# Weight tiles that begin where the activations begin, and four other starts for the seven products

## The chip, the cores and the metric

The kernel runs on one core of a Trainium2 chip. The metric is the device time of one execution in microseconds. The kernel before has a median of 2064.72 us over 3 runs (2064.69 to 2067.99).

## The reference

Two layers of a decoder trunk work on 512 tokens of width 1024 in float32. Each layer has three sub-layers between RMS norms: a SwiGLU FFN of width 2816, a mixer with a gated linear recurrence and a windowed attention, and a second FFN.

```python
for l in range(DEPTH):
    gn = norm_gains[l]
    h = rms_norm(x, gn[0])
    x = x + 0.5 * rms_norm(swiglu(h, w_ffn1_gate[l], w_ffn1_up[l], w_ffn1_down[l]), gn[1])
    h = rms_norm(x, gn[2])
    proj = h @ w_in[l]
    ...
    y_hg = hgrn2_mixer(hq, hf, hi, hg, lb_all[l], hgrn_head_gain[l]) @ w_branch_hgrn[l]
    y_at = swa_sink_attention(aq, ak, av, attn_sinks[l]) @ w_branch_attn[l]
    mixed = jax.nn.sigmoid(gate_a) * y_hg + jax.nn.sigmoid(gate_b) * y_at
    x = x + rms_norm(mixed @ w_out[l], gn[3])
    h = rms_norm(x, gn[4])
    x = x + 0.5 * rms_norm(swiglu(h, w_ffn2_gate[l], w_ffn2_up[l], w_ffn2_down[l]), gn[5])
```

`swiglu(h, g, u, d)` is `(silu(h @ g) * (h @ u)) @ d`. Nearly all of the arithmetic is in these products with weights.

## The kernel before

**Precision.** The matmul engine takes its operands as `float32r`, which rounds a float32. So every operand is split into two parts: `hi` is the rounded value, and `lo` is what rounding left over. A product is then three matmuls that add up in one accumulator (`mm3`): stationary hi with moving hi, stationary hi with moving lo, stationary lo with moving hi. All three go through `mm` on line 114, which is why the profile puts them on one line.

**Tiles.** Activations lie in `s` tiles (`big()`, line 62), 61 slots of 128 partitions by 2048 bytes. Weights arrive from memory in `w` tiles of 128 by 1024 elements. A *weight item* is one such tile, or a sum of parts of two, split into a `whi` and a `wlo` tile. There are six slots for each of these two, of 4096 bytes in a partition. Constants have a pool of their own, `cp`, that lies ahead of all of these. A tile keeps its place in the partition, and a slot is handed on in rotation, so a tile's address modulo 256 follows from what is allocated ahead of it.

**The stream of weights.** `Stream` (line 156) holds the list of all items in the order in which they are used. `split` (line 322) and `quarter` (line 255) make an item: ScalarE copies the weight to `hi`; `lo` is then made in one of two ways. Either VectorE subtracts (`wlo` on lines 294 and 362), or ScalarE writes the negative of the weight to `lo` (line 357) and a transfer issued by GpSimd adds the weight to `hi`'s negative in place (line 360). The kinds of item are:

- `u`, `v`: one plain tile. In most of its uses a 128-column block of it is the stationary operand, and 512 columns of activations stream. In the `rows` items of the down projections and of the output projection it is the other way round: activations are stationary, and 512 columns of weights stream.
- `a`, `b`, `c`, `d`: made by `pairs` out of two tiles. They serve `sevenths` (line 1031), which computes a 2 by 2 block product with seven block products instead of eight. There a weight block is stationary and 256 columns of activations stream. Four of these items hold the seven weight blocks of a pair: `a`, `b` and `c` two each, and `d` one.
- `p1` to `p7`: the quarter items of the down projections, where the same scheme is used with weights streaming, 512 columns at a time.

An FFN begins with a few columns done plainly (`quad`, `project`), goes on with pairs (`fast`, line 1074), and ends with `down`. The first FFN has 15 pairs, each of the other three has 19. A pair is 84 matmuls of 256 columns. The mixers use `pairs` through `gates` (line 186), four pairs in each layer. `ahead` (line 372) makes items up to four ahead of the one in use, never more than six at a time, and TensorE's program order is written out by hand. A matmul waits for its weight load, and that waits for the item.

**Constants that the change touches.** `gh` and `grows` (lines 1544 and 1552) hold the norms' gains while they are turned into rows, once, early in the program. `lbmx` holds a maximum for the recurrence's lower bounds. The activation on line 138 makes ScalarE load its function before it is needed; its result, in a tile named `warm`, is not used.

The item as it is made before:

```python
it.hi = sb.tile([P, D], F32R, tag="whi", name=nm("whi"), bufs=WS)
it.lo = sb.tile([P, D], F32R, tag="wlo", name=nm("wlo"), bufs=WS)
```

Of the kernel before, what the change touches and what calls it, by code (L numbers as in the profile page):

```python
# [8 lines left out]
F32R = mybir.dt.float32r  # L9
I32 = mybir.dt.int32  # L10
AF = mybir.ActivationFunctionType
# [4 lines left out]
P = 128  # L16
D = 1024
S = 512
DEPTH = 2
KT = D // P  # L20
TT = S // P
D_FF = 2816
FT = D_FF // P
H = 4
# [12 lines left out]
W32, WS, AHEAD, TAIL, FIRST, EARLY, LATE = 4, 6, 3, 4, 7, 4, 8  # L37
TURN = 0
SEVEN = 16
ORDER = ("p1", "p3", "p7", "p2", "p6", "p5")  # L40
HEADS = (0, 4, 1, 5, 2, 6, 3, 7)

# [2 lines left out]
def trunk(ctx: ExitStack, tc: tile.TileContext, xin, wall, gains, lbT, hgain, sinks, c_dist, c_mask, c_ident, out):  # L45
    nc = tc.nc
    cp = ctx.enter_context(tc.tile_pool(name="cp", bufs=1))
    sb = ctx.enter_context(tc.tile_pool(name="sb", bufs=1))
# [9 lines left out]
    def nm(s):  # L58
        seq[0] += 1
        return f"{s}_{seq[0]}"  # L60

    def big(dt=F32, shape=None):
        return sb.tile(shape or [P, S], dt, tag="s", name=nm("s"), bufs=SLOTS)

    def small(shape, tag, bufs=4, dt=F32):
        return sb.tile(shape, dt, tag=tag, name=nm(tag), bufs=bufs)
# [7 lines left out]
    def const(shape, name, dt=F32):  # L74
        return cp.tile(shape, dt, tag=name, name=name)
# [3 lines left out]
    class Order:  # L79
        def __init__(self):  # L80
            self.t = 0.0
            self.rest = 0.0
            self.cos = []
# [51 lines left out]
    nc.vector.memset(ones, 1.0)  # L135
    eps_t = const([P, 1], "eps_t")
    nc.vector.memset(eps_t, EPS)
    nc.scalar.activation(out=small([P, 1], "warm", 2), in_=eps_t, func=AF.Copy, scale=eps_t)


    p = aux()
# [8 lines left out]
    class Item:  # L150


        def __init__(self, kind, u, left=8):
            self.kind, self.u, self.left = kind, u, left

    class Stream:
        def __init__(self):
# [16 lines left out]
            self.n += n  # L174
            self.wall += n

        def pairs(self, n):

            for _ in range(n):
                self.items += [Item("a", self.n), Item("b", self.n), Item("c", self.n), Item("d", self.n, 4)]  # L180
                for i in range(2):
                    self.src.setdefault(self.n + i, self.wall + i)
                self.n += 2
                self.wall += 2
# [70 lines left out]
        def quarter(self, it):  # L255

            q, u, v, h = it.q, it.u, it.u + it.n, (slice(0, S), slice(S, D))

            def sums(o, x, y, op):
                for c in range(2):  # L260
                    pin(nc.vector.tensor_tensor(o[c], x[c], y[c], op=op))  # L261

            def raw(i):
                self.load(i + 1)
                return [self.raw[i][:, c] for c in h]

            def leave(i):
                self.raw.pop(i)
                self.freed += 1
                self.load(self.freed + W32)  # L270

            if it.kind in ("p1", "p2"):
                w = raw((u if it.kind == "p1" else v) + q)
            elif it.kind in ("p3", "p5"):
                w = self.b22[q]
            elif it.kind == "p7":

                w = self.b12[q]
                if q == 0:
                    sums(w, w, self.b22[q], ALU.add)  # L280
            else:
                w = self.b12[q]
            it.hi = sb.tile([P, D], F32R, tag="whi", name=nm("whi"), bufs=WS)
            it.lo = sb.tile([P, D], F32R, tag="wlo", name=nm("wlo"), bufs=WS)
            for c in range(2):
                i = nc.scalar.copy(it.hi[:, h[c]], w[c])  # L286
                if self.pinned:
                    pin(i)
            if it.kind == "p7" and q + 1 < it.n:
                sums(self.b12[q + 1], self.b12[q + 1], self.b22[q + 1], ALU.add)  # L290
            elif it.kind == "p6":
                sums(self.b22[q], self.b22[q], w, ALU.add)
            for c in range(2):
                pin(nc.vector.tensor_tensor(it.lo[:, h[c]], w[c], it.hi[:, h[c]].bitcast(F32), op=ALU.subtract))  # L294
            if it.kind == "p7":

                sums(w, raw(u + q), w, ALU.subtract)
                leave(u + q)
            elif it.kind == "p5":
                self.b22[q] = None  # L300
                if q + 1 < it.n:
                    sums(self.b12[q], raw(v + q), self.b12[q], ALU.add)
                    leave(v + q)
            elif it.kind == "p4":
                self.b12[q] = None
                if q == 0:
                    i = it.n - 1
                    sums(self.b12[i], raw(v + i), self.b12[i], ALU.add)
                    leave(v + i)
            self.done += 1  # L310
            self.flight += 1
# [10 lines left out]
        def split(self):  # L322
            it = self.items[self.done]
            if it.kind[0] == "p":
                return self.quarter(it)
            u, last = it.u, it.kind in "uvd"
            self.load(u + (1 if it.kind in "uv" else 2))
            it.hi = sb.tile([P, D], F32R, tag="whi", name=nm("whi"), bufs=WS)
            it.lo = sb.tile([P, D], F32R, tag="wlo", name=nm("wlo"), bufs=WS)
            w, h = self.raw[u], (slice(0, D // 2), slice(D // 2, D))  # L330
            cols = (slice(0, D),)
            if it.kind == "u" and u < 2:
                cols = h
            if it.kind in "bcd":
                v = self.raw[u + 1]
            if it.kind == "b":

                self.t13 = sb.tile([P, D], F32, tag="tt", name=nm("tt"), bufs=2)
                pin(nc.vector.tensor_tensor(self.t13[:, h[0]], w[:, h[0]], v[:, h[0]], op=ALU.add))
                pin(nc.vector.tensor_tensor(self.t13[:, h[1]], v[:, h[0]], v[:, h[1]], op=ALU.add))  # L340
                w = self.t13
                self.product()
            elif it.kind == "c":

                t = sb.tile([P, D], F32, tag="tt", name=nm("tt"), bufs=2)
                pin(nc.vector.tensor_tensor(t[:, h[0]], self.t13[:, h[0]], v[:, h[1]], op=ALU.add))
                pin(nc.vector.tensor_tensor(t[:, h[1]], t[:, h[0]], w[:, h[1]], op=ALU.add))  # L347
                w = t
            elif it.kind == "d":
                w = v  # L350
                cols = h[1:]
            for c in cols:
                i = nc.scalar.copy(it.hi[:, c], w[:, c])  # L353
                if u < 6 or self.pinned or self.tight:
                    pin(i)
                if it.kind in "vad":
                    i = nc.scalar.mul(it.lo[:, c], w[:, c], -1.0)  # L357
                    if self.pinned or self.tight:
                        pin(i)
                    nc.gpsimd.dma_start(it.lo[:, c].bitcast(F32), w[:, c], accum_op=ALU.add)  # L360
                else:
                    self.hold(nc.vector.tensor_tensor(it.lo[:, c], w[:, c], it.hi[:, c].bitcast(F32), op=ALU.subtract))  # L362
            self.done += 1
            self.flight += 1
            if last:
                nu = u + (1 if it.kind in "uv" else 2)
                for i in range(u, nu):
                    self.raw.pop(i)
                    self.freed += 1
                self.load(self.freed + W32)  # L370
# [38 lines left out]
    ws = Stream()  # L409
# [1064 lines left out]
    for l in range(DEPTH):  # L1474
        for n in (0, 2, 4):
            if n == 2:
                ws.plain(4, "v")
                ws.plain(2 * H + 2 + 8 + LATE * 3 // 2)
                for _ in range(KT - LATE // 2):
                    ws.gates()  # L1480
                ws.rows(KT, False)
            else:
                p = FIRST if l + n == 0 else 3
                ws.plain(4, "v" if l and not n else "u")
                ws.plain(min(2 * p, 8) - 4)
                ws.plain(max(2 * p - 8, 0), "v")
                ws.pairs(FT - p)
                ws.rows(FT, True)
    pre = First()
    for k in range(KT):  # L1490
# [27 lines left out]
        pre.square(k)  # L1518
    lb = const([P, DEPTH, H], "lb")
    oml = const([P, DEPTH, H], "oml")  # L1520
    mx = const([P, H], "lbmx")
    ex = const([P, DEPTH, H], "lbex")
    sm = const([P, H], "lbsm")
    cum = const([P, H], "lbcum")
# [1 line left out]
    def gain_rows():  # L1526
# [14 lines left out]
        nc.vector.tensor_tensor(cum, ex[:, 0, :], ex[:, 1, :], op=ALU.add)  # L1541
        nc.vector.tensor_tensor(lb[:, 1, :], cum, ex[:, 0, :], op=ALU.subtract)
        nc.vector.tensor_scalar(oml, lb, -1.0, 1.0, op0=ALU.mult, op1=ALU.add)
        t = const([P, DEPTH, 6, KT], "gh")
        pin(nc.vector.tensor_scalar(t, g_sb, 1.0, None, op0=ALU.mult))
        for n in (1, 5):
            nc.vector.tensor_scalar(t[:, :, n, :], t[:, :, n, :], 0.5, None, op0=ALU.mult)
# [1 line left out]
        p = aux()  # L1549
        nr = DEPTH * 6 * KT  # L1550
        transpose(p[:nr, :P], t.rearrange("p a b c -> p (a b c)"))
        r = const([nr, P], "grows")
        nc.scalar.copy(r, p[:nr, :P])
        nc.sync.dma_start(rows_d, r)

# [88 lines left out]
```

## Time and profile before

| | |
|---|---|
| median of 3 runs | 2064.72 us |
| the profiled execution | 2063.08 us |
| its span, first to last instruction | 2061.3 us |
| mean granted clock of the matmul engine | 0.999 |
| matmuls, weight loads | 13531 each |
| matmuls that read a weight tile | 12096 |
| read from memory | 213.43 MB |

The profile names the engines PE (matmuls), PEld (the loads of stationary operands, which run beside the matmuls), DVE (VectorE), ACT (ScalarE), POOL (GpSimd) and SP (transfers). A row of groups gives line, engine, operation, the tile written, the tiles read, partitions and shape, the count, the busy time in us and the mean duration of one in ns, and then the idle time ahead of them with what ended it. For matmuls the stationary size comes as 128*128 and the streamed one behind it; `acc` and `aux` are accumulators, and "acc<-s,whi" means that `s` streams against a loaded `whi`, "acc<-whi,s" the reverse. A row of waits gives who waited, for whom, the total in us, how often, and the longest. A row of windows gives a stretch of the span, its length, the busy time and count, the granted clock and the load on the transfers. A row of the timeline gives start, length, engine, line and operation; "x2" means that two in a row are merged. Times in windows and timeline count from the start of the span.

### The profile page before, as it was taken

To read this page: it belongs to the slowest core of one execution; us is meant where nothing else is said; L and a number is where in the kernel's file an instruction comes from. 1 tells how busy PE (TensorE), PEld (TensorE's weight loads), DVE (VectorE), ACT (ScalarE), POOL (GpSimd) and SP (SyncE) were. 2 spreads that over 40 slices of the span, in tenths; PEclk is the share of its full clock that TensorE was granted. 3 is DMA by queue.
4 is the path that set the end of the run, shared out by engine and by line. 5 is a ranking of instruction groups with operands and counts; after the bars stand their busy time and mean duration, and the time that the engine had idled before them with its cause. 6 is when DMAs were issued, how large, how long until landed. Compare 5 with 4: busy or idle time off the path is not lost. (4 is left out here: it accounts for less than half of the span.)

```text
span 2061.3 us, 36501 instructions
## 1 busy us (share of the span) xinstructions
PE 2047.5 (99%) x13531; PEld 1818.4 (88%) x13531; DVE 1625.6 (79%) x2894; ACT 1252.2 (61%) x2213; POOL 268.2 (13%) x318
## 2 busy tenths in 40 slices
PE   9999999999999999999999999999999999999998
PEld 7899988877888899997899998888778989999977
DVE  5887888767777787888988878987676858788888
ACT  7566687447355556657866666864554545666684
POOL 0111141000000011113201111400000100111140
PEclk9999999999999999999999999999999999999999
DMA  8587797321237358778757888872122563778794
GB/s 253 148 189 189 171 206 222 125 72 62 81 94 210 116 135 193 190 197 204 193 161 184 189 193 204 176 232 91 62 72 62 136 192 95 184 188 189 187 197 123
DMA packets 166802, 328.07 MB, mean 159 GB/s; under 512 B 19072, under 2 KB 85088, under 8 KB 166624
## 3 DMA queue, kind: packets, MB, share of 16 engines
q1 hardware_dynamic: 122416, 228.16, 33.0%
q0 software_dynamic: 44064, 97.54, 28.5%
q8 instruction: 106, 1.74, 0.4%
q14 instruction: 72, 0.59, 0.1%
q10 hardware_dynamic: 144, 0.05, 0.0%
HBM read 213.43 MB, written 14.73 MB: 111 GB/s over the span
## 5 line engine op out<-in xcount | busy, mean ns | idle before, releaser
L114 PE MATMUL acc<-s,whi 128*128 128x256 f32 (+1 forms) x4976 | 1030.4, 306 | 0.4 <-ACT whi L353 0.4
L114 PEld LDWEIGHTS acc<-s,whi 128*128 128x128 f32 x4976 | 792.5, 188 | 52.9 <-issue 3.2
L114 PE MATMUL acc<-s,wlo 128*128 128x256 f32 (+1 forms) x2488 | 760.4, 306 | 3.5 <-DMA wlo<-w 3.1
L114 PEld LDWEIGHTS acc<-s,wlo 128*128 128x128 f32 x2488 | 468.3, 188 | 32.4 <-DMA wlo<-w 5.6
L114 PE MATMUL acc<-whi,s 128*128 128x512 f32 x1360 | 446.5, 397 | 2.2 <-DVE s L432 1.3
L353 ACT CAST whi<-w 128x1024 fp32r<-128x1024 f32 (+1 forms) x310 | 286.8, 929 | 157.2 <-PE acc L114 103.2
L353 ACT CAST whi<-tt 128x1024 fp32r<-128x1024 f32 x160 | 167.9, 1050 | 249.5 <-DVE tt L347 155.9
L360 POOL DMA_DIRECT2D wlo<-w x178 | 154.3, 869 | 1242.9 <-ACT wlo L357 530.1
L114 PEld LDWEIGHTS acc<-whi,s 128*128 128x128 f32 x1360 | 255.6, 188 | 62.9 <-issue 3.2
L362 DVE TENSOR_TENSOR wlo<-tt,whi 128x1024 fp32r<-128x1024 f32 x160 | 196.0, 1225 | 131.6 <-ACT whi L353 130.5
L114 PE MATMUL acc<-wlo,s 128*128 128x512 f32 x680 | 267.7, 394 | 0.4 <-DVE wlo L294 0.3
L114 PE MATMUL aux<-s,whi 128*128 128x256 f32 (+1 forms) x1296 | 229.8, 280 | 0.0
L362 DVE TENSOR_TENSOR wlo<-w,whi 128x1024 fp32r<-128x1024 f32 (+1 forms) x132 | 157.5, 1206 | 75.3 <-ACT whi L353 70.2
L114 PEld LDWEIGHTS aux<-s,whi 128*128 128x128 f32 x1296 | 197.2, 188 | 1.1 <-issue 0.5
L114 PE MATMUL aux<-s,wlo 128*128 128x256 f32 (+1 forms) x648 | 180.9, 279 | 0.0
L114 PEld LDWEIGHTS acc<-wlo,s 128*128 128x128 f32 x680 | 128.0, 188 | 30.1 <-DVE wlo L294 2.8
L357 ACT ACTIVATE wlo<-w 128x1024 fp32r<-128x1024 f32 (+1 forms) x178 | 153.6, 863 | 0.2 <-PE acc L114 0.2
L114 PE MATMUL aux<-whi,s 128*128 128x512 f32 x432 | 145.4, 394 | 0.0
L443 POOL DMA_DIRECT2D s<-s x128 | 111.3, 972 | 217.4 <-ACT s L431 98.6
L114 PEld LDWEIGHTS aux<-s,wlo 128*128 128x128 f32 x648 | 121.8, 188 | 0.4
L294 DVE TENSOR_TENSOR wlo<-s,whi 128x512 fp32r<-128x512 f32 x160 | 102.8, 686 | 9.8 <-ACT whi L286 6.3
L431 ACT CAST s<-s 128x512 fp32r<-128x512 f32 (+1 forms) x140 | 70.8, 548 | 45.1 <-DVE s L490 39.5
(186 smaller groups left out, 2469.5 us busy)
## 6 DMA issues: line engine op xcount, KB each, us to landing
w<-wall SPq DMA_DIRECT2D x267, 512.0 KB, 4.4
wlo<-w POOLq DMA_DIRECT2D x98, 512.0 KB, 5.3
w<-wall SPq DMA_DIRECT2D x224, 128.0 KB, 3.5
wlo<-w POOLq DMA_DIRECT2D x80, 256.0 KB, 3.3
s<-wall SPq DMA_DIRECT2D x128, 128.0 KB, 4.4
s<-s POOLq DMA_DIRECT2D x64, 256.0 KB, 4.7
x_d<-s SPq DMA_DIRECT2D x48, 256.0 KB, 3.9
s<-x_d SPq DMA_DIRECT2D x48, 256.0 KB, 5.0
```

The source lines that it names most:

```text
L114: nc.tensor.matmul(o, lhsT, rhs, start=start, stop=stop)
L294: pin(nc.vector.tensor_tensor(it.lo[:, h[c]], w[c], it.hi[:, h[c]].bitcast(F32), op=ALU.subtract))
L353: i = nc.scalar.copy(it.hi[:, c], w[:, c])
L357: i = nc.scalar.mul(it.lo[:, c], w[:, c], -1.0)
L360: nc.gpsimd.dma_start(it.lo[:, c].bitcast(F32), w[:, c], accum_op=ALU.add)
L362: self.hold(nc.vector.tensor_tensor(it.lo[:, c], w[:, c], it.hi[:, c].bitcast(F32), op=ALU.subtract))
L431: (hold or ws.hold)(nc.scalar.copy(hi, src))
L443: nc.gpsimd.dma_start(lo.bitcast(F32), src, accum_op=ALU.add)
```

## The change

The tiles `whi` and `wlo` become 64 elements (256 bytes) longer, and an item uses 1024 elements of them from an offset `at` on. The offset is 0 for plain and quarter items, 16 elements (64 bytes) for the pairs of the mixers, and 24, 8, 20 and 12 elements (96, 32, 80 and 48 bytes) for the pairs of the four FFNs in the order of the program. So that the longer tiles fit, `gh` and `grows` take slots of the activations instead of places among the constants. The warm-up writes its result to `lbmx`, which is now allocated near the start, and not to a `warm` tile.

```diff
+ASIDE = 16
+PLACES = (24, 8, 20, 12)
...
-    nc.scalar.activation(out=small([P, 1], "warm", 2), in_=eps_t, func=AF.Copy, scale=eps_t)
+    mx = const([P, H], "lbmx")
+    nc.scalar.activation(out=mx[:, :1], in_=eps_t, func=AF.Copy, scale=eps_t)
...
     class Item:
-        def __init__(self, kind, u, left=8):
-            self.kind, self.u, self.left = kind, u, left
+        def __init__(self, kind, u, left=8, at=0):
+            self.kind, self.u, self.left, self.at = kind, u, left, at
...
-        def pairs(self, n):
+        def pairs(self, n, at=ASIDE):
             for _ in range(n):
-                self.items += [Item("a", self.n), Item("b", self.n), Item("c", self.n), Item("d", self.n, 4)]
+                self.items += [Item(k, self.n, 4 if k == "d" else 8, at) for k in "abcd"]
...
-            it.hi = sb.tile([P, D], F32R, tag="whi", name=nm("whi"), bufs=WS)
-            it.lo = sb.tile([P, D], F32R, tag="wlo", name=nm("wlo"), bufs=WS)
+            it.hi, it.lo = (sb.tile([P, D + 64], F32R, tag=t, name=nm(t), bufs=WS)[:, it.at : it.at + D] for t in ("whi", "wlo"))
...
-                ws.pairs(FT - p)
+                ws.pairs(FT - p, PLACES[2 * l + n // 4])
...
-    mx = const([P, H], "lbmx")
...
-        t = const([P, DEPTH, 6, KT], "gh")
+        t = big()[:, : DEPTH * 6 * KT].rearrange("p (a b c) -> p a b c", a=DEPTH, b=6)
...
-        r = const([nr, P], "grows")
+        r = big()[:nr, :P]
```

The line that makes `hi` and `lo` stands in both `quarter` and `split`. The shapes, the order and the number of all operations stay as they were.

More of the change, by code (lines that the diff above doesn't have):

```diff
@@ L327, in split @@
             self.load(u + (1 if it.kind in "uv" else 2))
-            it.hi = sb.tile([P, D], F32R, tag="whi", name=nm("whi"), bufs=WS)
-            it.lo = sb.tile([P, D], F32R, tag="wlo", name=nm("wlo"), bufs=WS)
+            it.hi, it.lo = (sb.tile([P, D + 64], F32R, tag=t, name=nm(t), bufs=WS)[:, it.at : it.at + D] for t in ("whi", "wlo"))
             w, h = self.raw[u], (slice(0, D // 2), slice(D // 2, D))
```

## The prediction

> **What bounds the kernel now.** I read the head of the page first, then the waits of the matmul engine, then its groups by shape, and last its rate in single stages.
>
> ```profile
> span 2061.3 us, 36501 instructions
> ...
> PE 2047.5 (99%) x13531; PEld 1818.4 (88%) x13531; DVE 1625.6 (79%) x2894; ACT 1252.2 (61%) x2213; POOL 268.2 (13%) x318
> ...
> PEclk9999999999999999999999999999999999999999
> ```
>
> The matmul engine is busy for 99% of the span, and its clock is granted in full in every slice. Its waits, all together:
>
> ```profile
> PE acc L114 <- DMA wlo<-w: 3.1, 5, 1.2
> PE acc L114 <- DVE s L432: 1.3, 2, 0.7
> PE aux L114 <- DVE eps_t L137: 1.1, 1, 1.1
> PE acc L124 <- DVE s L862: 1.0, 2, 0.5
> PE aux L114 <- DVE wlo L294: 0.9, 3, 0.3
> PE acc L114 <- ACT whi L286: 0.9, 1, 0.9
> PE acc L114 <- ACT whi L353: 0.4, 1, 0.4
> PE acc L114 <- DVE wlo L294: 0.3, 1, 0.3
> ```
>
> That is 9.0 us in all. No other engine sets the end. What remains is how many matmuls there are, which the change leaves alone, and how long each takes from its start to the next one's. Three kinds carry nearly all of it:
>
> ```profile
> L114 PE MATMUL acc<-s,whi 128*128 128x256 f32 x3840 | 669.0, 278 | 0.0
> L114 PE MATMUL acc<-s,wlo 128*128 128x256 f32 x1920 | 536.0, 279 | 3.4 <-DMA wlo<-w 3.1
> L114 PE MATMUL acc<-whi,s 128*128 128x512 f32 x1360 | 446.5, 397 | 2.2 <-DVE s L432 1.3 <-ACT whi L286 0.9
> L114 PE MATMUL acc<-s,whi 128*128 128x512 f32 x1136 | 361.6, 399 | 0.4 <-ACT whi L353 0.4
> ```
>
> The operand named first streams. So 256-column matmuls stream activations against a loaded weight tile, 512-column ones stream either. The duration of one (278 ns) holds its tail, which the next one overlaps, so I take the rate from stages: time over count.
>
> ```profile
> 90.20:238.60 148.40, 148.40 (x1261) 1.00 0.79 188
> 735.30:921.20 185.90, 183.71 (x1597) 1.00 0.79 189
> 1069.60:1253.80 184.20, 183.63 (x1597) 1.00 0.79 189
> 1752.10:1937.30 185.20, 184.54 (x1597) 1.00 0.79 189
> 100.00:230.00 130.00, 130.00 (x1106) 1.00 0.80 190
> 1144.00:1184.00 40.00, 40.00 (x355) 1.00 0.81 190
> ```
>
> The first four rows are the seven-product stages of the four FFNs in order (window, its length, matmul busy time and count; about two of each count are cut at an edge). The last two are stretches inside the first and the third FFN. 130.0 us over 1104 is 117.8 ns, and 40.0 over 353 is 113.3. **The same shape runs at two cadences**, 4.4 ns apart, and each lasts for hundreds of matmuls. The first FFN is long throughout (148.4 us over 1260 is 117.8). The other three average 115.1, 115.1 and 115.6: mostly short, with long stretches and the restarts after their stalls.
>
> 512-column matmuls that stream weights have two cadences too. Here is the timeline in a late stretch, in the first down projection, and for a stretch that streams activations:
>
> ```profile
> 658.72 0.39 PE L114 MATMUL aux<-wlo,s 128*128 128x512 f32 x1
> ...
> 660.78 0.39 PE L114 MATMUL acc<-wlo,s 128*128 128x512 f32 x1
> ```
> ```profile
> 258.72 0.63 PE L114 MATMUL acc<-whi,s 128*128 128x512 f32 x2
> ...
> 260.12 0.63 PE L114 MATMUL acc<-whi,s 128*128 128x512 f32 x2
> ```
> ```profile
> 23.74 0.40 PE L114 MATMUL acc<-s,wlo 128*128 128x512 f32 x1
> ...
> 25.14 0.40 PE L114 MATMUL acc<-s,wlo 128*128 128x512 f32 x1
> ```
>
> Between the starts lie 9, 6 and 6 matmuls: 2.06/9 is 229 ns, 1.40/6 is 233.3, and 1.40/6 again. I found no stretch of activation-streaming 512s faster than 233.3.
>
> **The change, part by part.** *Addresses.* By the order of allocation, activation slots begin 64 bytes past a multiple of 256 before and weight tiles 128 past one: a distance of 64. After it two constants (384 and 512 bytes) leave the pool, the first `warm` slot comes later, and weight tiles grow to 4352 bytes, 17 times 256. Activations and weight tiles then both begin 192 past a multiple of 256. The distance becomes 0 for plain items and the quarter items of the down projections, stays 64 for the mixer's `gates`, and becomes 96, 32, 80 and 48 for the seven products of the four FFNs. The trace holds one distance only, so no row prices the others. I bound them by the cadences it does show.
>
> *Seven products* (1260 and three times 1596 matmuls). All short: 1260 x 113.3 ns is 142.8 us, against 148.4, a gain of 5.6. Each later stage would be 180.8 us against 183.7, 183.6 and 184.5: gains of 2.9, 2.8 and 3.7, which can't all be had, since a restart costs something at any cadence. Together at best -15.0 us. All long: 187.9 us for each later stage, +4.2, +4.3 and +3.4, together +11.9. A worse cadence than any shown, one more step of 4.4 ns on 6048 matmuls, would be another +26.6; I keep that outside the range. I take the middle of the two, half long and half short: 145.6 for the first stage (-2.8) and 184.4 for the others (+0.7, +0.8, -0.1), **-1.4 us**. Nothing in the trace says which distance favours which cadence.
>
> *512s that stream weights* (quarter items, `rows`; 1360 with 680, 432 and 216 by the groups, 2688). Their tiles start at a multiple of 128 before, and 64 past one after: the place of the activations, whose 512s never ran short. If the start of the streamed operand decides, these lose their short cadence. The first FFN's 480 are long already. The other 2208 (three times 480, four times 192 in the mixers) range from 229 to 233.3. If all were at 229, going long would cost 2208 x 4.3 ns, or 9.5 us; stalls and the mixer's stretches put part of them at 233.3 today, so I take **+8 us**. The other bound is a gain: 2688 at 229 at all times, about -3 us, and the 1728 activation-streaming 512s (1136, 568 and 24) going from 233.3 to 229, -7.4 us, for the distance of 0 changes for them as well.
>
> *Weight loads.* A load is as long as ever in elements; what a start off 64 bytes costs is not in the trace. It would come out in the cadence just bounded, because a 256-column matmul and the next load run side by side.
>
> *The copies into the tiles.* The three writers of a tile keep their sizes:
>
> ```profile
> L357 ACT ACTIVATE wlo<-w x178: 624/1047/1072, 30.2 to 1928.5; 128x1024 fp32r<-128x1024 f32 x98, 128x512 fp32r<-128x512 f32 x80
> L360 POOL DMA_DIRECT2D wlo<-w x178: 862/862/1159, 31.6 to 1929.4; - x178
> ...
> DMA to landing us min/median/max: 3.2/5.0/9.5
> ```
>
> ScalarE and VectorE copies are hidden by the four items the stream works ahead. The accumulating transfer is the one that already comes late: 3.1 us of matmul time waits for it, five times. If starts at 48 and 80 bytes slow it, the waits could double, +3; if not, 0. I take **+1**.
>
> *Constants.* `gh` and `grows` now use two of 61 slots for some 20 us early on, and the warm-up of ScalarE writes `lbmx`. Nothing waits for these; their cover is the full matmul queue. Without it, two slots less could delay a slot's reuse once, by under the 0.7 us of the longest wait for `s`. I take **+1** for this with restarts that fall elsewhere.
>
> The sum is -1.4 + 8 + 1 + 1 = +8.6 us on the profiled execution's 2063.1 (span 2061.3 and 1.8 around it), or 2071.7. That execution lies 1.6 under the median of 2064.7, so the forecast is **2073.3**.
>
> **Where a page speaks against it.** One matmul shows what a load beside it costs. It is the second of the pair at 900.05, the last before a stall:
>
> ```profile
> 900.05 0.39 PE L114 MATMUL acc<-s,whi 128*128 128x256 f32 x2
> 901.62 0.39 PE L114 MATMUL acc<-s,wlo 128*128 128x256 f32 x1 [1.18 <-DMA wlo<-w]
> ```
> ```profile
> 899.94 0.30 PEld L114 LDWEIGHTS acc<-s,whi 128*128 128x128 f32 x2
> 901.62 0.19 PEld L114 LDWEIGHTS acc<-s,wlo 128*128 128x128 f32 x1 [1.38 <-DMA wlo<-w]
> ```
>
> No load ran beside it, and the pair is still 0.39 long, as pairs with loads in that stretch are. The Trainium skill says the same in "TensorE: Matmul & The Clock Gate", Part 2, step by step: the engine has two independent SBUF read ports, and loading the next weights takes no read bandwidth from the running matmul. By that rule the distance between weights and activations can't matter, and the sum would be nothing but the two small terms. The trace agrees for this one matmul, but the rule doesn't explain two cadences of one shape.
>
> **The rivals.** *Faster:* the new distances are ones at which the streams don't disturb each other. For it: two cadences show that there is something to win, and the first FFN has 5.6 us of it. Against: three of four stages are mostly short already. The products alone give -15.0, with the 512s' gains (-3 and -7.4) -25.4: 2049.7 down to 2039.3. I put it at 2050.
>
> *Nothing changes:* addresses don't decide, the cadence is set anew at each stall as before, and the change doesn't do what its offsets are for. For it: the matmul at 900.05, and both cadences at one distance. Against: stretches of hundreds of matmuls keep their cadence, so something fixed holds it. Time: 2064.7, give or take 3.
>
> *Slower on all counts:* the seven products lose the short cadence at distances that are no multiple of 64, from the first matmul of the second FFN on, where the short one rules today. +11.9 + 8 + 2 is +21.9, or 2086.6; it decides once more than half of a stage is long. For it: short stretches exist at the one aligned distance that the trace has. Against: that same distance gave the first FFN no short matmul.
>
> **How the numbers follow.** Forecast 0.40, faster 0.35, nothing changes 0.12, slower on all counts 0.13. The forecast's own range is 2067 to 2080. For 8 in 10 I go to 2045, which cuts off the case in which all gains meet, and to 2092, which holds slower on all counts but not an unseen cadence. A difference under 0.2% (4.1 us) can't be told from none in this kernel. The forecast's lower end lies within that, which moves 0.02 to no change; a fifth case of small gains moves 0.01 more from no change to faster. So slower 0.51, same 0.13, faster 0.36.
>
> **What would show it.** The head of the page should keep the counts of matmuls and loads, and the waits of the matmul engine should stay near 9 us. Right would be the four product stages at about 146 and three times 184 us, and 512s that stream weights at 233.3 ns wherever they run. If these stay at 229 in the late stretches, the +8 falls. If a product stage shows a cadence that is neither 113.3 nor 117.8, the bounds were too narrow, and its distance tells for which offset. If the waits for `wlo` grow in the last two FFNs alone, whose starts are 80 and 48 bytes, the transfers are what the offsets cost. An unchanged mix of cadences in every stage would make the whole account wrong.

## The result, and the profile after

The changed kernel takes 2058.32 us (median of 5 runs, 2057.63 to 2058.70), against 2064.72 for the kernel before on the same chip (5 runs, 2060.07 to 2067.99). The ratio is 0.9969 with an interval of 0.9956 to 0.9983: 6.4 us, or 0.3%, faster, where 2073.3 was forecast. The profiled execution took 2058.61 us. The head of its page:

```profile
span 2056.8 us, 36503 instructions
...
PE 2048.5 (100%) x13531; PEld 1841.9 (90%) x13531; DVE 1624.7 (79%) x2894; ACT 1252.8 (61%) x2213; POOL 267.6 (13%) x318
...
PEclk9999999999999999999999999999999999999999
```

The matmul engine still sets the end, at the full clock and with the same 13531 matmuls. Its waits, all of them:

```profile
PE aux L116 <- DVE eps_t L139: 1.1, 1, 1.1
PE acc L126 <- DVE s L863: 1.0, 2, 0.5
PE acc L116 <- DMA wlo<-w: 1.0, 2, 0.5
PE acc L116 <- ACT whi L354: 0.9, 1, 0.9
```

They went from 9.0 to 4.0 us. The waits for `wlo` on the transfer fell from 3.1 to 1.0, those on VectorE's `wlo` and on line 432's `s` are gone. The transfer into `wlo` itself is as it was, now with starts of 48 and 80 bytes among its targets:

```profile
L361 POOL DMA_DIRECT2D wlo<-w x178: 859/859/1089, 31.4 to 1924.6; - x178
...
DMA to landing us min/median/max: 3.2/5.0/9.1
```

The main part can't be seen in the groups, since the duration of one matmul holds a tail that the next one overlaps. It is in the rate of single stages. The view of windows (start and end, length, busy time and count of matmuls, clock, load on the transfers), first the four stages of seven products, then the four down projections:

```profile
88.70:236.50 147.80, 147.80 (x1261) 1.00 0.79 191
729.50:919.10 189.60, 189.15 (x1597) 1.00 0.78 187
1065.40:1254.80 189.40, 189.40 (x1598) 1.00 0.79 188
1747.20:1936.10 188.90, 188.90 (x1598) 1.00 0.79 188
236.50:347.10 110.60, 109.10 (x482) 1.00 0.82 202
919.10:1029.50 110.40, 108.90 (x482) 1.00 0.83 204
1254.80:1365.20 110.40, 108.90 (x482) 1.00 0.83 202
1936.10:2047.60 111.50, 109.19 (x482) 1.00 0.70 166
```

Before, the product stages took 148.4, 185.9, 184.2 and 185.2. Over 1260 and 1596 matmuls, the rows are now 117.3 ns (at 96 bytes), 118.8 (32), 118.7 (80) and 118.4 (48). Without the second row's two stalls its cadence is 118.3. Before, the later three were mixes of 113.3 and 117.8; now none is. The down projections of before, which the prediction did not show, in the same view:

```profile
238.60:352.10 113.50, 112.00 (x481) 1.00 0.80 197
921.30:1034.10 112.80, 110.99 (x481) 1.00 0.82 202
1253.90:1368.90 115.00, 111.38 (x481) 1.00 0.83 202
1937.40:2052.20 114.80, 111.44 (x482) 1.00 0.69 166
```

Together 456.1 us before and 442.9 after: -13.2. The timeline of after shows why, in the first down projection, and below it in a stretch where activations stream:

```profile
239.62 0.39 PE L116 MATMUL acc<-wlo,s 128*128 128x512 f32 x1
...
242.34 0.39 PE L116 MATMUL acc<-wlo,s 128*128 128x512 f32 x1
```
```profile
21.68 0.39 PE L116 MATMUL acc<-s,wlo 128*128 128x512 f32 x1
...
25.76 0.39 PE L116 MATMUL acc<-s,wlo 128*128 128x512 f32 x1
```

Between the starts lie 12 and 18 matmuls: 2.72/12 and 4.08/18 are both 226.7 ns. That is less than the 229 and 233.3 of before, and it holds for either operand streaming.

Two stages with 256 columns got slower. The windows of an FFN's first plain columns (192 matmuls, now at distance 0) and of one pair of the mixers (84, still at 64), before and then after:

```profile
352.30:376.30 24.00, 22.50 (x193) 22.28 (x192) 1.00 0.72 226
593.80:603.30 9.50, 9.50 (x85) 9.46 (x84) 1.00 0.67 144
```
```profile
347.30:372.00 24.70, 23.20 (x193) 22.98 (x192) 1.00 0.73 224
586.70:596.60 9.90, 9.90 (x86) 9.86 (x85) 1.00 0.63 138
```

The whole account, added up from the time between each matmul's start and the next one's. Gaps over 126 ns (256 columns) or 245 ns (512 columns) count as stalls and are left out of the cadence, but not out of the sums:

| matmuls | ns, before | ns, after | us, before to after |
|---|---|---|---|
| seven products, 6048 of 256 | 117.8, then 114.3 to 114.6 | 117.3, 118.3, 118.7, 118.3 | +11.8 |
| 512s that stream weights, 2688 | 230.2 on the mean | 227.2 | -14.4, of which stalls and their gaps 34.9 to 23.2 |
| 512s that stream activations, 1728 | 233.3 | 227.9 | -9.1 |
| first columns of an FFN, 960 of 256 | 116.2 | 119.9 | +3.5 |
| the mixers' pairs, 672 of 256 | 113.4 | 117.3 | +3.3 |

Steady stretches of 512s in after are at 226.7 for both streams, and the mixers' pairs at 117.8, one of their eight blocks apart (113.6). The sum is -4.8, and all other matmuls together took 0.4 us more; the span went from 2061.3 to 2056.8, -4.5.

### The profile page after: what moved, and what is told of

Its sections match the earlier page's. It is cut to its first block, busy times and chain, and to the rows that moved or that the text cites. A ratio compares the mean times of both kernels' runs of the same rounds, so it can differ in the third digit from the quotient of the medians.

```text
span 2056.8 us, 36503 instructions
## 1 busy us (share of the span) xinstructions
PE 2048.5 (100%) x13531; PEld 1841.9 (90%) x13531; DVE 1624.7 (79%) x2894; ACT 1252.8 (61%) x2213; POOL 267.6 (13%) x318
## 4 chain that ended last, share of the span: by engine, by line
PE 78%; issue 14%; DVE 3%; DMA 2%; ACT 1%; POOL 0%; SPq 0%; POOLq 0%; DVEq 0%; ACTq 0%
PE acc L116 59%; PE aux L116 17%; PE aux L126 1%; DMA wlo<-w 1%; DVE wlo L296 1%; DMA w<-wall 1%; DVE s L264 1%; DVE wlo L363 0%; DVE s L433 0%; DVE s L968 0%; ACT s L442 0%; PE acc L126 0%; POOL wlo L361 0%; ACT whi L288 0%; DMA s<-xin 0%
## 5 line engine op out<-in xcount | busy, mean ns | idle before, releaser
L116 PE MATMUL acc<-s,whi 128*128 128x256 f32 (+1 forms) x4976 | 1042.3, 307 | 0.9 <-ACT whi L354 0.9
L116 PEld LDWEIGHTS acc<-s,whi 128*128 128x128 f32 x4976 | 800.7, 189 | 47.7 <-issue 3.2
L116 PE MATMUL acc<-whi,s 128*128 128x512 f32 x1360 | 441.4, 393 | 0.0
L116 PE MATMUL aux<-s,whi 128*128 128x256 f32 (+1 forms) x1296 | 235.7, 282 | 0.0
```

Source lines behind the costliest of these rows:

```text
L116: nc.tensor.matmul(o, lhsT, rhs, start=start, stop=stop)
```

## The experiments

The question was what sets a cadence: the distance between the starts of the two operands, the streamed operand's own start, or nothing that is fixed. All edits but the last are against the changed kernel. Apart from one version with six runs, each ran once, beside the kernel before on the same chip. That kernel took 2060.70 us beside the first four experiments; 2063.02 beside those at 16 to 192 bytes, at 8 to 56 bytes and the one that enters at the short cadence; 2061.67 (median of 11) beside those at 4 to 120 bytes, with 8 everywhere and with 8 and 0; and 2064.43 beside the last. By itself it spreads over 2059.0 to 2066.7, so single times here tell less than cadences do. Distances are the bytes from the start of an activation slot to the start of a weight tile, modulo 128.

### Distance 0 everywhere

```diff
-ASIDE = 16
-PLACES = (24, 8, 20, 12)
+ASIDE = 0
+PLACES = (0, 0, 0, 0)
```

> All weight items at distance 0 from the activations (modulo 256 bytes), the pairs too. Distance theory: the cadence of a matmul is set by the distance between the starts of its two operands, so the seven products and the mixers' pairs run at the 119.9 ns that the 256-column matmuls at distance 0 show in the changed kernel, against 117.3 to 118.7 there; 512s stay at 226.7. 6720 matmuls by about 1.7 ns: 11 us slower than the changed kernel, about 2070. Start theory (each operand's own start decides): the streamed activations have not moved, so the products stay at 117 to 119 and the time at 2058. Redraw theory (only the phases after stalls were drawn anew): a mix of 113.3 and 117.8, anything from 2035 to 2060.

Measured: 2070.36 us, as the theory of distance had it. The windows of its first two product stages:

```profile
89.30:240.40 151.10, 151.10 (x1262) 1.00 0.78 187
733.70:925.20 191.50, 191.50 (x1598) 1.00 0.78 186
```

151.1/1260 and 191.5/1596 are 119.9 and 120.0, and the other two stages are 191.5 as well. The mixers' pairs run at 119.9 too, and the 512s stay at 226.7. So at distance 0 all 256-column matmuls, in six kinds of place, run at one cadence (119.8 to 120.0): slow for 256 columns, fast for 512.

### The products at distance 64

```diff
-PLACES = (24, 8, 20, 12)
+PLACES = (16, 16, 16, 16)
```

> The products of all four FFNs at 64 bytes, the distance of the kernel before, all else as changed. Distance theory: products show 113.3 and 117.8 and nothing else. If they enter at 117.8, as six of the mixers' seven undisturbed pair stages at 64 do in the changed kernel, they stay there until a stall: about 2056; if the stalls flip them to 113.3, down to 2035. Redraw theory: the same mix in any case, so this run cannot tell it apart alone, but 118.3 and 118.7 should then show here too. Start theory: weight starts of 64 are as in the mixers' pairs, 117.8 throughout, 2056.

Measured: 2055.67 us. The stages took 148.4, 188.0, 185.0 and 188.0. The third changes within:

```profile
1064.00:1084.00 20.00, 20.00 (x173) 20.00 (x172) 1.00 0.74 173
...
1140.00:1160.00 20.00, 20.00 (x179) 20.00 (x178) 1.00 0.81 188
```

Some three of each count are cut at the edges, which makes these 117.8 and 113.3. Only those two cadences occur at 64, as before the change. The change of cadence sits at a stall: 456 ns lie between the start of this matmul and that of the one ahead of it, the cadence is long up to there and short from there on.

```profile
1123.54 0.39 PE L116 MATMUL acc<-s,wlo 128*128 128x256 f32 x1 [0.17 <-DMA wlo<-w]
```

The distance gives the choice of two, and something else takes it.

### Plain and quarter items back at 64

```diff
-        def __init__(self, kind, u, left=8, at=0):
+        def __init__(self, kind, u, left=8, at=16):
```

> Plain and quarter items at 64 bytes as before the change, the products of the FFNs at 96, 32, 80 and 48 as changed. Distance theory: 512s go back to 233.3 where activations stream and to 229 or 233.3 where weights stream, which is 9 and 8 us slower by the two stage sums, and the stalls behind them may come back, 12 more: 2075 to 2087. Start theory: only the 512s that stream weights change, 8 us: 2066. Redraw theory: no systematic change, 512s mixed.

Measured: 2066.28 us, which is the number of the theory of own starts, though the cadences are those of the theory of distance. Without their stalls, the activation-streaming 512s are back at 233.2 (+8.9 us against after) and the weight-streaming ones at 229.9 on the mean (+7.4), with both cadences of before. Two of the four down projections:

```profile
922.10:1033.50 111.40, 109.90 (x482) 1.00 0.83 202
1258.40:1371.90 113.50, 112.00 (x482) 1.00 0.81 197
```

What the expectation left out is that the same edit takes the first columns of the FFNs back to 116.2 (-3.5) and lets the mixers' pairs run at 113.4 again (-3.0), and that no more stalls came than in after (22.6 us of gaps in the weight-streaming 512s, 23.2 in after). The products had stayed slow, which may be why. Its time alone would have pointed to the wrong theory.

### Both operands moved by 64

```diff
+    const([P, 16], "shift")
```

It is an unused constant of 64 bytes ahead of all tiles: every start moves, no distance does.

> 64 unused bytes ahead of all tiles: activations and weights both begin 64 bytes later, at a multiple of 256, and every distance stays. Distance theory: the same cadences in every stage as in the changed kernel, 226.7, 119.9, 117.3, 118.3, 118.7, 118.3, and 2058.5 within 2. Start theory: 512s and products change, by several us either way. Redraw theory: another mix of cadences.

Measured: 2058.03 us, and the product stages:

```profile
88.80:236.60 147.80, 147.80 (x1262) 1.00 0.79 191
729.10:918.00 188.90, 188.90 (x1598) 1.00 0.77 188
1064.60:1254.00 189.40, 189.40 (x1598) 1.00 0.78 189
1746.40:1935.30 188.90, 188.90 (x1598) 1.00 0.77 189
```

They are those of after, cadence by cadence, and so are the 512s (226.7) and the first columns (119.9). The one difference is at 64: all eight blocks of the mixers' pairs ran at 117.8 here, where one of after's, with a stall at its start, ran at 113.6. A theory in which the own start of either operand decides, and one in which each layout draws its cadences anew, would both have shown something else: by their own start, modulo 128, the first stage's weight tiles would now be where the second's were in after, and the reverse, and each would have taken over the other's cadence. Both fall. In every kernel here activations begin at a multiple of 64; whether a move of both by less than 64 would change anything was not tried.

### More distances

```diff
-PLACES = (24, 8, 20, 12)
+PLACES = (4, 28, 32, 48)
```

> The four FFNs' products at 16, 112, 128 and 192 bytes, all else as changed. If the distance counts modulo 128, the third FFN at 128 runs at the 120.0 ns of distance 0 and the fourth at 192 at 117.8 or 113.3, as 64 does; if it counts modulo 256, they may show anything. 16 and 112 have not been seen: between 113.3 and 120. The time follows from the four stages: 1260 or 1596 matmuls by what each cadence differs from 117.3, 118.3, 118.7 and 118.3; about 2057 if all lie near 118.

```diff
-PLACES = (24, 8, 20, 12)
+PLACES = (2, 6, 10, 14)
```

> Products at 8, 24, 40 and 56 bytes, not multiples of 16. If distances act in steps of 16 bytes, they run like their neighbours, 117 to 120; if each byte distance has a cadence of its own, new values. One below 113.3 would show that a start off 16 bytes pays. About 2058 if all lie between 117.3 and 120.

```diff
-PLACES = (24, 8, 20, 12)
+PLACES = (1, 3, 18, 30)
```

> Products at 4, 12, 72 and 120 bytes, all else as changed. The runs so far give 120.0 ns at 0, 115.6 at 8, 118.3 at 16, 119.2 at 24 and 117.8 at 56 and at 192. If the dependence repeats modulo 128 and is smooth near 8, 4 and 12 lie between 115.6 and 120; 72 (8 past 64) and 120 (8 short of 128) tell whether 8 bytes past or short of a multiple of 64 is what helps: 115.6 or less at one of them, near 118 at the other. About 2055 to 2062.

Measured: 2063.13, 2062.78 and 2059.48 us. The first kernel's third and fourth stages are at 128 and 192 bytes:

```profile
1067.90:1259.50 191.60, 191.60 (x1597) 1.00 0.78 186
1752.10:1940.00 187.90, 187.90 (x1596) 1.00 0.79 189
```

The counts hold one or two cut matmuls, so these are 120.0 and 117.8: 128 acts as 0 does and 192 as the longer one of 64, so the distance counts modulo 128, as far as these two pairs can tell. The expectations of about 2057 and 2058 for the first two were missed by 6 and 5 us: the first has two stages at 120.0 ns, the second one at 121.9. The second kernel's first and second stages, at 8 and 24 bytes:

```profile
88.30:234.00 145.70, 145.70 (x1262) 1.00 0.79 190
728.50:923.10 194.60, 194.60 (x1598) 1.00 0.77 183
```

That is 115.6 ns at 8, and 121.9 at 24, the worst of all. (The expectation of the third kernel gives 119.2 for 24; that is the cadence at 40.) Of the third kernel's, neither 72 nor 120 is short, so being 8 off a multiple of 64 is not what helps at 8. All distances that ran, for 256 columns:

| bytes | 0 | 4 | 8 | 12 | 16 | 24 | 32 | 40 |
|---|---|---|---|---|---|---|---|---|
| ns | 120.0 | 118.3 | 115.6 | 116.7 | 118.3 | 121.9 | 118.3 | 119.2 |

| bytes | 48 | 56 | 64 | 72 | 80 | 96 | 112 | 120 |
|---|---|---|---|---|---|---|---|---|
| ns | 117.8 or 118.3 | 117.8 | 113.3 or 117.8 | 118.3 | 118.7 | 117.3 | 120.0 | 119.4 |

### Entering the products at the short cadence

With the products at 64, the last plain item ahead of them is put at 64 too, and so is the one behind each of the mixers' pairs, so that the products, and every pair of a mixer but its first, are entered from matmuls at their own distance.

```diff
-            self.plain(1)
+            self.plain(1, at=ASIDE)
...
-                ws.plain(min(2 * p, 8) - 4)
-                ws.plain(max(2 * p - 8, 0), "v")
+                ws.plain(min(2 * p, 8) - 4 - (p == 3))
+                ws.plain(int(p == 3), at=ASIDE)
+                ws.plain(max(2 * p - 9, 0), "v")
+                ws.plain(int(p > 4), "v", ASIDE)
```

> Products at 64 as in the run of that name, and the last plain item ahead of them, and the one behind each of the mixers' pairs, at 64 as well. Theory that the stage ahead decides which of the two cadences of distance 64 is entered: from 512s at 64 the products enter at 113.3 in the later three FFNs and in the mixers, as before the change, until a stall; the first FFN may stay long. 4788 and 672 matmuls by up to 4.4 ns less than 117.8, 24 us, less what the stalls of faster products cost, about 4 us a stage by the kernel before: 2035 to 2048. Rival, that the cadence at 64 is a matter of where stalls fall: 2055 as in the run with the products at 64 alone.

Measured: 2057.69 us. All four product stages were entered at 117.8; the second dropped to 113.3 in its middle alone (115.7 on the mean), and three of the mixers' eight blocks ran at 113.4 to 113.6. The theory fell, as far as the products go.

The traces hold more on the choice at 64 than this run alone. In the product stages and mixers' pairs that ran at 64, in the kernel before, the changed one and all the runs above, 114 stretches of 24 or more matmuls lie between stalls (a gap over 126 ns) or the ends of a stage. But for a few matmuls right behind a stall, each keeps one cadence throughout, so a change inside a stage falls at a stall. Of the stalls with such a stretch on both sides, 24 came at the short cadence, and 17 of them left it short and 7 long; 6 came at the long one, and all of them left it short. In the mixers it also shows what carries a cadence over: between two pairs lie only the 24 matmuls of one plain item. In this run that item was at 64, and the short cadence that began at a stall in the second block held in the third and fourth. With that item at 0 (after, the products at 64, and the kernels at 16 to 192 and 4 to 120), the block that followed such a stall was long again each time, five times in all. What decides after a stall, and at entry into the later FFNs of the kernel before, stays open.

### Distance 8 everywhere, and 8 for 256 columns alone

Of the distances tried, 8 is the one at which 256 columns run steadily fast. First every item is put there:

```diff
-ASIDE = 16
-PLACES = (24, 8, 20, 12)
+ASIDE = 2
+PLACES = (2, 2, 2, 2)
...
-        def __init__(self, kind, u, left=8, at=0):
+        def __init__(self, kind, u, left=8, at=2):
```

> All weight items at 8 bytes: 512s too. The products should show 115.6 in all four FFNs, as the first one did at 8, if the distance alone decides. For the 512s the distance theory has no value yet: 226.7 if 8 bytes do as well as 0, up to 233.3 if only 0 is good; that is 0 to 30 us for 4400 of them. Products, mixers' pairs and the halved 256-column matmuls gain about 22 against the changed kernel: 2036 if 512s keep 226.7, 2066 if they all go to 233.3.

Measured: 2076.18 us, worse than any bound. The 256s ran at 115.6 throughout and activation-streaming 512s at 230.7, but a down projection looks like this in the timeline:

```profile
239.71 0.64 PE L116 MATMUL aux<-whi,s 128*128 128x512 f32 x2
...
241.63 0.40 PE L116 MATMUL acc<-wlo,s 128*128 128x512 f32 x1
```

With 8 matmuls between, 1.92/8 is 240 ns, a cadence not seen until then. It is 13.3 over distance 0. All weight-streaming 512s together, the mixers' too, ran at 239.2 on the mean and took 625.1 us without their stalls, 30.2 more than in after. The best steady distance for one shape is the worst seen for another. But the roles differ too: counted from the streamed operand to the loaded one, 8 is 8 where activations stream and -8, or 120 modulo 128, where weights do. Streaming weights were tried at 0, 8 and 64 alone.

So the two are separated: 8 for the items whose matmuls have 256 columns, 0 for those with 512.

```diff
-ASIDE = 16
-PLACES = (24, 8, 20, 12)
+ASIDE = 2
+PLACES = (2, 2, 2, 2)
...
-        def plain(self, n, kind="u"):
-            self.items += [Item(kind, self.n + i) for i in range(n)]
+        def plain(self, n, kind="u", at=0):
+            self.items += [Item(kind, self.n + i, at=at) for i in range(n)]
...
-                ws.plain(4, "v")
+                ws.plain(4, "v", ASIDE)
...
-                ws.plain(4, "v" if l and not n else "u")
+                ws.plain(4, "v" if l and not n else "u", ASIDE if l + n else 0)
```

> The 512s at 0, all 256-column matmuls (products, mixers' pairs, and the first four items of each halved stage) at 8. Distance theory: 512s 226.7, 256s 115.6, which against the changed kernel is 2.2 us in the first product stage, 5.2, 5.0 and 4.5 in the others, 4.1 in the halved stages and 1.2 in the mixers, 22 in all: 2036, or up to 2048 if faster products bring back the waits for transfers and for VectorE that the kernel before had. Redraw theory: no better than the changed kernel, 2058.

Measured: 2052.12 us (6 runs, 2051.51 to 2052.85) against 2061.67, a ratio of 0.9949 with an interval of 0.9934 to 0.9964, and above the 2036 to 2048 expected. This version beats the kernel before beyond noise; its runs also lie below those of after, though the two were not timed side by side. The cadences are as expected, 115.6 and 226.7, but 16 of the 22 us were not had. Two product stages and the two down projections after them:

```profile
727.80:913.90 186.10, 185.54 (x1598) 1.00 0.79 188
1062.20:1248.40 186.20, 185.33 (x1598) 1.00 0.79 189
...
913.90:1027.10 113.20, 110.61 (x481) 1.00 0.83 202
1248.40:1361.40 113.00, 110.33 (x481) 1.00 0.83 203
```

At 115.6 ns without a stall, a stage of 1596 is 184.5 us, so 1.6 and 1.7 went into restarts, and 1.5 in the last FFN. The four down projections took 453.8 us, 10.9 more than in after at the same cadence. With the 4.8 that is 15.7, the missing 16. Gaps over 245 ns among the weight-streaming 512s went from 70 (23.2 us) to 111 (42.8 us). Of the matmul engine's waits, these name who is late:

```profile
PE acc L116 <- DVE s L433: 2.5, 4, 0.7
PE acc L116 <- DMA wlo<-w: 1.9, 3, 0.8
PE aux L116 <- DVE wlo L296: 1.2, 4, 0.3
...
PE acc L116 <- DVE wlo L296: 0.9, 4, 0.3
```

It is VectorE and the accumulating transfer, which supply operands. These rows hold 6.5 us; that the rest of the 15.7 is the restarts that follow such waits is not shown. The kernel with distance 8 everywhere is the control. Its product stages have the same 115.6, but its 512s are slower, and it had 75 such gaps (25.5 us) and 0.9 us of waits for the transfer. So faster products alone didn't bring the stalls; they came when both kinds of stage were short.

### Two distances in one product

```diff
-PLACES = (2, 2, 2, 2)
+PLACES = ((2, 0), (0, 2), (2, 16), (16, 2))
...
-            it.hi, it.lo = (sb.tile([P, D + 64], F32R, tag=t, name=nm(t), bufs=WS)[:, it.at : it.at + D] for t in ("whi", "wlo"))
+            it.hi, it.lo = (sb.tile([P, D + 64], F32R, tag=t, name=nm(t), bufs=WS)[:, a : a + D] for t, a in zip(("whi", "wlo"), it.at if isinstance(it.at, tuple) else (it.at, it.at)))
```

It starts from the version just shown, and `whi` and `wlo` of an item begin at the two places named. The second line of the edit stands in both `quarter` and `split`.

> As the kernel with 512s at 0 and 256s at 8, but the two tiles of a product item at different distances: (hi, lo) at (8, 0), (0, 8), (8, 64) and (64, 8) bytes in the four FFNs. Two of three matmuls load a hi tile. If each matmul has the cadence of its own loaded operand's distance, the stages run at (2 x 115.6 + 120.0) / 3 = 117.0, (2 x 120.0 + 115.6) / 3 = 118.5, and between 114.8 and 116.3 and between 114.1 and 117.0 for the last two, since 64 has two cadences. If the phase that one matmul leaves acts on the next, the stages show cadences outside of these means. About 2052 to 2058.

Measured: 2052.09 us, and in the first two product stages:

```profile
88.60:237.00 148.40, 148.40 (x1262) 1.00 0.79 190
727.50:916.30 188.80, 188.33 (x1597) 1.00 0.79 189
```

Both run at 117.8, where a mean of the matmuls' own distances (two with `whi`, one with `wlo`) would be 117.0 for the first and 118.5 for the second. The third and fourth, with 8 and 64, were at 115.7 and 116.7, inside the ranges expected. A cadence is not simply each matmul's own cost by its own distance. Whether the distances that precede it take part, or the tile that is loaded beside its stream, was not tried.

## Why the prediction was wrong

**The step that failed** is the one that began "If the start of the streamed operand decides, these lose their short cadence", and made +8 us for the weight-streaming 512s. It took a start for the cause; the run with both operands moved shows that it is a distance. At distance 0 those matmuls did not go long. They went to 226.7, below the 229 that the prediction had set as the best there is, and with their stalls they gave 14.4 us. The gain of the activation-streaming 512s was noted in the same paragraph as a bound (-7.4) and left out of the sum; it was -9.1. Both bounds came from cadences that one distance, 64, had shown, and the change left that distance.

**The seven products** were put at -1.4 and cost +11.8. That this is nearly the "all long" bound of +11.9 is an accident of sizes. They run at 118.3 to 118.7 in three stages, a little over the long cadence. And the bound was taken from the later stages' busy times, which leaves their 3.4 us of idle time as it was, where only 0.5 us of it remained. The prediction had named what this means: a cadence neither 113.3 nor 117.8 shows that the bounds were too narrow, and the distance tells for which offset.

**Left out of the sum** were the first columns of the FFNs, which moved from distance 64 to 0 (+3.5), and the mixers' pairs, which stayed at 64 (+3.3). In after the latter run at the long one of the two cadences of 64, and at the short one when plain items are at 64: the items between them decide whether a short cadence is carried over, as the runs at 64 show.

**Transfers and constants** (+1 and +1) were the wrong way round. Waits fell by 5.0 us, and the landings in the rows of the transfer are as they were, 5.0 us at the median with starts of 48 and 80 bytes among them. Slower products leave more time for the next items. That this is the reason is an inference, supported by the version at 8 and 0, in which shorter products and 512s brought the waits for `wlo` and `s` back.

**The rivals.** "Faster" had the sign right and a wrong account. It expected most of its 15 us from the products, and all of the gain came from the 512s, which gave 23.5 and lost 18.7 to the 256s. "Nothing changes" is excluded by the ratio's interval and by the new cadences. Its account, a cadence set anew at each stall, was seen at distance 64 alone. Weighed against the trace there was the statement of the Trainium skill in "TensorE: Matmul & The Clock Gate", Part 2, step by step, of two independent read ports, from which the prediction concluded that distance could not matter. The runs speak against that conclusion: between two kernels that differ in nothing but the products' offsets, the second FFN's stage moves from 116.7 (at 12) to 121.9 ns (at 24). The pair at 900.05 that seemed to support it is one matmul with its stage's usual duration; it shows no cadence. Nor did it run free of a load: the row of loads beside it lasts to 900.24, past the start of the pair's second matmul.

**What stays open** is the mechanism in the chip, which of 113.3 and 117.8 follows a stall or an entry at distance 64, and why 8 bytes is good for 256 columns and bad for streamed weights. That the kernel before spreads over 7.7 us on one chip (11 runs), and the versions with little or nothing at 64 over 1.1 (after, 5 runs) and 1.3 (8 and 0, 6 runs), would fit a choice that falls anew in each execution; only one execution of each was profiled, so this was not seen.

## What to carry to other kernels

Where matmuls run back to back and nothing else waits, take the cadence of each stage (time over count) and not the duration of a single matmul, and try the distance between the operands' starts as a tuning parameter of its own, separately for each shape and for each operand that streams. Measure the distances, since a bound drawn from the one that a trace shows does not hold for another. And ahead of counting a faster cadence as a gain, ask whether the engines that supply operands can follow: here 6 us came out of 22.

## What was not expected of the hardware

- The cadence of these `float32r` matmuls depends on the distance of their operands' starts, as far as tried modulo 128 bytes: 113.3 to 121.9 ns for 256 columns, 226.7 (distance 0) to 240.0 (8) for 512 that stream weights, and 226.7 (0), 230.7 (8) and 233.3 (64) for 512 that stream activations.
- It is not only a matter of multiples: 24 bytes is the worst of sixteen distances for 256 columns, and 8 the best steady one, though neither is a multiple of 32.
- At 0, 8, 32, 80 and 96 bytes the cadence, stalls left out, came out the same to 0.1 ns in each product stage that ran there. At 64 there are two, 4.4 ns apart, and each is kept from one stall to the next, for up to 1596 matmuls; at 48, 117.8 and 118.3 came in different kernels.
